# A decoder block on one core: the up projection by Strassen's seven products, and what is rearranged around it

## The chip, the cores and the metric

The kernel runs on one core of a Trainium2 chip. The metric is the device time of one execution in microseconds (us). Its engines are named as in the profile: PE is TensorE's matmul, PEld its weight load, DVE is VectorE, ACT is ScalarE, POOL is GpSimd, SP is SyncE, which issues most of the loads. "L127" is line 127 of the kernel before.

## What is computed

One decoder block on 512 tokens of width 1024 in float32: a gated merge of differential attention and causal pooling, an output projection, and an MLP with squared ReLU.

```python
h = rmsnorm(x, norm_attn_g[l])
u = h @ w_in[l]
u_q, u_k, u_v, u_pool, u_gate = jnp.split(u, splits, axis=-1)
...
a = diff_attention(q, k, v, positions, lam, subln_g[l], lam_init)
p = multiscale_pool(u_pool, w_pool[l], pool_scale[l])
gates = jax.nn.sigmoid(u_gate.reshape(B, S, N_BRANCHES, D_MODEL))
merged = gates[:, :, 0] * a + gates[:, :, 1] * p
x = x + (merged @ w_out[l]).astype(x.dtype)
h2 = rmsnorm(x, norm_mlp_g[l])
z = jnp.square(jax.nn.relu(h2 @ w_up[l]))
x = x + (z @ w_down[l]).astype(x.dtype)
return rmsnorm(x, final_norm_g)
```

`w_up` is 1024 x 4096 and `w_down` 4096 x 1024.

## The kernel before

**Numbers in two parts.** Every matmul takes operands of the type fp32r. To keep the accuracy, each operand is split: a high part (a cast on ACT) and a low part, the rest (a subtraction, mostly on DVE). A product is then three matmuls: high by high, high by low, low by high. Weights come as raw tiles of 128 x 1024 float32 (512 KB) through the SP queue (`load_w`, L95, three raw buffers with the tag `wr`), and `split_w` (L107) makes `wh` and `wl` (four buffers each). `get_w` (L112) can also make the low part with a DMA that accumulates ("dma": a cast, a negated copy and a transfer on POOL's queue that adds the raw weights).

**Order.** The program is written stage by stage. A planner orders the instructions of each engine by a simulated timeline and sets all waits; `after(later, earlier)` (L59) adds an edge to the planner's order and no wait on the chip.

**Attention.** Per head, projections, scores, softmax and values follow one another (`qk`, `attn`), and between them "fillers" (pooling and gate projections, `pool` at L409 and `gate` at L442) run. `merge` (L446) joins a head's output, its gates and its pooling product `pp`. `pool` loads its small weight `wpr` (L434) into a buffer with the tag `sq`, which the squares and norms of the heads use as well. Pooling, gate and `pp` products share three PSUM banks in turn.

**Output projection.** `w_out` comes in eight tiles in two halves (L546 to L563). After the second half of a tile of 128 tokens, the row scale is worked out, h2 is made (`h2`, all four token tiles), transposed on PE, and split into `x1gh` and `x1gl` (L571, L572).

**MLP.** D_FF is worked through in four quarters of 1024 columns; in each, `up(q)` (L606) and then `down(q)` (L620).

- `up` is a plain product: eight column tiles of 128, each 24 matmuls (`mm3`, L123) of 512 tokens, so 192 matmuls a quarter. In quarter 0 the first two tiles run in halves of 256 tokens, since the later tokens' h2 comes late. `z_of` (L588) takes relu and square on ACT, makes the forms of z that Strassen's scheme (Winograd's variant) wants (S1 to S4 by subtractions on DVE) and splits all seven into `zfh` and `zfl`, which hold seven forms each.
- `down` is already done by seven products over blocks (tokens in two halves, D_FF quarter in two halves, model width in two halves). Each product is 24 matmuls of 512 columns. The sums of weight blocks are made in DRAM-to-SBUF transfers that accumulate (`plus`, L638, on POOL's queue). The order is A11, S3, S2, S1, A12, S4, A22. Some products go onto banks that hold an earlier one (`onto`): S2 onto A11's, S4 onto S1's, A22 onto S3's. In between stands at least one other product. `to_x1` (L656) adds or subtracts the two banks of a product to `x1` on DVE. A sum U over the quarters is kept and added in the last one.
- In the last quarter the final norm is folded into the end (L686 to L730): the last product A22 runs in three pieces (`cols`, L708), 512, 256 and 256 columns, the second and third in the two halves of one bank.

## Time and profile before

| | us |
|---|---|
| three runs | 697.95, 695.3, 697.5; median 697.5 |
| the profiled execution | 697.38 |
| its span | 695.6 |
| last matmul of the last product starts | 688.30 |

The profile shows one execution. Its span runs from the first to the last instruction; the execution's own time has 1.8 us around it. Busy times of PE are not pure work: matmuls overlap, so that the distance between two starts, not the length of one, tells what a matmul costs.

### The profile page before, as it was taken

To read this page: it belongs to the slowest core of one execution; us is meant where nothing else is said; L and a number is where in the kernel's file an instruction comes from. 1 tells how busy PE (TensorE), PEld (TensorE's weight loads), DVE (VectorE), ACT (ScalarE), POOL (GpSimd) and SP (SyncE) were. 2 spreads that over 40 slices of the span, in tenths; PEclk is the share of its full clock that TensorE was granted. 3 is DMA by queue.
4 is the path that set the end of the run, shared out by engine and by line. 5 is a ranking of instruction groups with operands and counts; after the bars stand their busy time and mean duration, and the time that the engine had idled before them with its cause. 6 is when DMAs were issued, how large, how long until landed. Compare 5 with 4: busy or idle time off the path is not lost.

```text
span 695.6 us, 8855 instructions
## 1 busy us (share of the span) xinstructions
PE 679.3 (98%) x3158; PEld 564.3 (81%) x3158; DVE 476.4 (68%) x834; ACT 420.0 (60%) x683; POOL 161.2 (23%) x151
## 2 busy tenths in 40 slices
PE   8999999999999999999999999999999999999995
PEld 7788878888888887787888888888888888888884
DVE  6953977789788875965385675555765567645785
ACT  7554487977986689674356644455434554355544
POOL 6101634264345525532300010000210011000100
PEclk9999999999999999999999999999999999999998
DMA  7534574426436365345943269823797249952523
GB/s 268 165 115 116 133 150 120 103 63 157 125 88 151 99 152 121 91 163 201 246 128 118 91 107 288 231 100 91 179 247 209 90 92 209 248 177 91 95 57 122
DMA packets 30140, 100.88 MB, mean 145 GB/s; under 512 B 3600, under 2 KB 4240, under 8 KB 30096
## 3 DMA queue, kind: packets, MB, share of 16 engines
q1 hardware_dynamic: 22464, 72.79, 30.0%
q0 software_dynamic: 7488, 27.27, 23.0%
q8 instruction: 25, 0.41, 0.2%
q10 hardware_dynamic: 144, 0.26, 0.1%
q14 instruction: 19, 0.16, 0.1%
HBM read 98.20 MB, written 2.10 MB: 144 GB/s over the span
## 4 chain that ended last, share of the span: by engine, by line
PE 78%; DVE 10%; ACT 6%; issue 2%; DMA 2%; POOL 1%; SPq 0%; DVEq 0%; ACTq 0%; POOLq 0%
PE pu L127 8%; PE pu L128 8%; PE pu L131 8%; PE m L652 7%; PE m L653 7%; PE m L651 7%; PE po L536 2%; PE po L537 2%; PE po L538 2%; DVE p L376 2%; PE q L127 2%; PE k L127 2%; PE k L128 2%; PE q L128 2%; PE q L131 2%
## 5 line engine op out<-in xcount | busy, mean ns | idle before, releaser
L127 PE MATMUL pu<-x1gh,wh_up 128*128 128x512 f32 (+1 forms) x272 | 101.0, 377 | 0.2 <-ACT x1gh L571 0.2
L128 PE MATMUL pu<-x1gl,wh_up 128*128 128x512 f32 (+1 forms) x272 | 101.1, 377 | 0.0
L641 POOL DMA_DIRECT2D wr_b<-w_dn x32 | 27.7, 927 | 299.7 <-DVE wl_t L109 228.5
L109 DVE TENSOR_TENSOR wl_up<-wr_up,wh_up 128x1024 fp32r<-128x1024 f32 x32 | 39.2, 1225 | 41.8 <-ACT wh_up L108 30.3
L131 PE MATMUL pu<-x1gh,wl_up 128*128 128x512 f32 (+1 forms) x272 | 64.0, 377 | 0.0
L108 ACT CAST wh_up<-wr_up 128x1024 fp32r<-128x1024 f32 x32 | 33.7, 1053 | 44.4 <-PE m L653 20.0
L127 PEld LDWEIGHTS pu<-x1gh,wh_up 128*128 128x128 f32 x272 | 51.0, 188 | 9.8 <-ACT x1gh L571 0.5
L128 PEld LDWEIGHTS pu<-x1gl,wh_up 128*128 128x128 f32 x272 | 51.2, 188 | 9.6 <-DVE x1gl L572 0.2
L131 PEld LDWEIGHTS pu<-x1gh,wl_up 128*128 128x128 f32 x272 | 49.2, 188 | 9.3
L108 ACT CAST wh_t<-wr_b 128x1024 fp32r<-128x1024 f32 x32 | 33.6, 1053 | 38.1 <-PE m L653 24.6
L109 DVE TENSOR_TENSOR wl_t<-wr_b,wh_t 128x1024 fp32r<-128x1024 f32 x32 | 38.9, 1224 | 22.8 <-ACT wh_t L108 13.2
L604 DVE TENSOR_TENSOR zfl<-zr,zfh 128x512 fp32r<-128x512 f32 (+1 forms) x32 | 34.9, 1091 | 26.8 <-ACT zfh L603 26.8
L651 PE MATMUL m<-wh_t,zfh 128*128 128x512 f32 x120 | 46.7, 389 | 0.0
L652 PE MATMUL m<-wl_t,zfh 128*128 128x512 f32 x120 | 46.7, 389 | 0.0
L653 PE MATMUL m<-wh_t,zfl 128*128 128x512 f32 x120 | 46.7, 389 | 0.0
L371 ACT ACTIVATE p<-p,st 128x128 f32<-128x128 f32 (+3 forms) x64 | 35.8, 560 | 17.6 <-DVE st L367 17.1
L603 ACT CAST zfh<-zr 128x512 fp32r<-128x512 f32 (+1 forms) x32 | 30.2, 944 | 23.6 <-DVE zr L601 16.6
L652 PE MATMUL m<-wl_b,zfh 128*128 128x512 f32 x96 | 37.3, 389 | 0.0
L653 PE MATMUL m<-wh_b,zfl 128*128 128x512 f32 x96 | 37.3, 389 | 0.0
L651 PE MATMUL m<-wh_b,zfh 128*128 128x512 f32 x96 | 37.2, 389 | 0.0
L376 DVE SCALAR_TENSOR_TENSOR p<-p,st 128x128 f32<-128x128 f32 (+3 forms) x32 | 28.9, 902 | 8.0 <-ACT p L375 8.0
L109 DVE TENSOR_TENSOR wl_b<-wr_b,wh_b 128x1024 fp32r<-128x1024 f32 x16 | 19.6, 1224 | 18.4 <-PE pu L131 9.9
(266 smaller groups left out, 1794.4 us busy)
## 6 DMA issues: line engine op xcount, KB each, us to landing
wr_b<-w_dn SPq DMA_DIRECT2D x32, 512.0 KB, 3.8
wr_up<-w_up SPq DMA_DIRECT2D x32, 512.0 KB, 6.2
wr_b<-w_dn POOLq DMA_DIRECT2D x32, 512.0 KB, 5.9
wr_q<-w_in SPq DMA_DIRECT2D x8, 512.0 KB, 3.2
wr_k<-w_in SPq DMA_DIRECT2D x8, 512.0 KB, 3.3
wr_ga<-w_in SPq DMA_DIRECT2D x8, 512.0 KB, 3.2
wr_gp<-w_in SPq DMA_DIRECT2D x8, 512.0 KB, 3.4
wl_ga<-w_in POOLq DMA_DIRECT2D x8, 512.0 KB, 5.7
```

Source lines behind the costliest of these rows:

```text
L108: ins = A.copy(out=hi[:, sl], in_=raw[:, sl])
L109: (eng or G).tensor_tensor(out=lo[:, sl], in0=raw[:, sl], in1=f(hi)[:, sl], op=ALU.subtract)
L127: T.matmul(acc, lhsT=hi[:, c], rhs=rh[:, k, :], start=k == 0, stop=False)
L128: T.matmul(acc, lhsT=hi[:, c], rhs=rl[:, k, :], start=False, stop=False)
L131: T.matmul(acc, lhsT=lo[:, c], rhs=rh[:, k, :], start=False, stop=k == NK - 1)
L371: A.activation(out=pr[:, c, :N], in_=pr[:, c, :N], func=AF.Exp, scale=-1.0, bias=st[:, c : c + 1], accum_out=st[:, 2 + c : 3 + c])
L376: V.scalar_tensor_tensor(out=pr[:, 0, :N], in0=pr[:, 0, :N], scalar=st[:, 4:5], in1=pr[:, 1, :N], op0=ALU.mult, op1=ALU.add)
L603: A.copy(out=zfh[:, sl, p, :], in_=F[:, sl])
L604: V.tensor_tensor(out=zfl[:, sl, p, :], in0=F[:, sl], in1=f(zfh)[:, sl, p, :], op=ALU.subtract)
L651: T.matmul(pa[a], lhsT=zh, rhs=hi[:, sl], start=p == 0 and onto is None, stop=False, skip_group_check=True)
L652: T.matmul(pa[a], lhsT=zh, rhs=lo[:, sl], start=False, stop=False, skip_group_check=True)
L653: T.matmul(pa[a], lhsT=zl, rhs=hi[:, sl], start=False, stop=p == 3 and stop, skip_group_check=True)
```

## The change

- **Up in quarters 1 to 3** is done by seven products as well. Both operands are cut in two by two blocks: h2 (features in two halves, tokens in two halves), and the quarter of `w_up` (features in two halves, columns in two halves). A product of blocks has 2 x 2 x 12 matmuls of 256 columns (tokens). `w_up` is laid out anew by the host for it. Quarter 0 stays a plain product (`up_plain`), with weights in the new layout.
- **Forms of h2.** The four combined forms S1 to S4 of h2 are made once, during quarter 0 (`forms_h2`), and kept with their splits in `gss`; the plain blocks are in `gab`.
- **Forms of weights.** `weights` serves both projections. It loads block 0 (`r11`) and block 1 (`al`), adds them on DVE (`ga`), and changes `ga` and `al` step by step by accumulating transfers. Splits go into a ring of three pairs (two in `wp`, the third in `bk`). For some forms the cast is put behind the first matmul of the product before (`hold`).
- **Forms of z** live in a ring of four buffers (`zform`) in place of seven. `up` makes z blocks by keeping, joining, relu and square, in five raw blocks `R`; the forms are split as they come, the last three (S4, S3, A22) when down's products have set a buffer free.
- **Down** runs in the order S1, A11, S2, A12, S4, S3, A22 with S2, S3 and A22 on A11's banks one after the other, and S4 on S1's. U is gone: each product is added to or subtracted from `x1` as it stands. A product runs over the token tiles outside and the four parts inside.
- **The end:** the pieces for tokens 0 to 255 are finished earlier; the third piece of the last product has a bank of its own.
- **Before the MLP:** `wpr` has a tag of its own; `pp` of heads 4 to 7 is put behind the sigmoid in the planner's order; the raw ring has two buffers, and a third from the attention pool while that is open; the constants come in two transfers; the even tiles of `w_out`, whose low parts POOL made before, get them by an accumulating transfer in the first half and on DVE in the second; h2 is kept for two token tiles.

```diff
     def load_w(src, name, nsplit=1, parts=None):
-        raw = wp.tile([P, 1024], F32, tag="wr", name=f"wr_{name}", bufs=3)
+        nraw[0] += 1
+        third = nraw[0] % 3 == 0 and ctx1_open
+        raw = (tp if third else wp).tile([P, 1024], F32, tag="wr3" if third else "wr", name=f"wr_{name}", bufs=1 if third else 2)
...
-        wr = tmp("sq", f"wpr{g}", (P, 256))
+        wr = tmp("wpr", f"wpr{g}", (P, 256), bufs=1)
...
-        T.matmul(p_, lhsT=wph[:, c], rhs=dh, start=True, stop=False)
+        first_ = T.matmul(p_, lhsT=wph[:, c], rhs=dh, start=True, stop=False)
+        if h > 3:
+            after(first_, sg)
...
-        w = get_w(w_out[0, kk], f"o0_{kk}", V if kk % 2 else None)
+        w = get_w(w_out[0, kk], f"o0_{kk}", V if kk % 2 else "dma")
...
+    def forms_h2():
...
+        def minus(x, y):
+
+            V.tensor_tensor(out=w, in0=x[0], in1=y[0], op=ALU.subtract)
+            V.tensor_tensor(out=u, in0=x[1], in1=y[1], op=ALU.subtract)
+            V.tensor_tensor(out=w, in0=w, in1=u, op=ALU.add)
+
+        def less(x):
+
+            V.scalar_tensor_tensor(out=w, in0=w, scalar=-1.0, in1=x[0], op0=ALU.mult, op1=ALU.subtract)
+            V.tensor_tensor(out=w, in0=w, in1=x[1], op=ALU.subtract)
+
+        def parts(form):
+            hi, lo = gf[form]
+            A.copy(out=hi, in_=w)
+            V.tensor_tensor(out=lo, in0=w, in1=f(hi), op=ALU.subtract)
+
+        minus(a11, a21)
+        parts(S3)
+        minus(a22, a21)
+        parts(S1)
+        less(a11)
+        parts(S2)
+        less(a12)
+        parts(S4)
...
+        r11, al, ga = raw(0), raw(1, "wal", bk), raw(None, "wga", bk)
+        for c in range(2):
+            V.tensor_tensor(out=ga[c], in0=r11[c], in1=al[c], op=ALU.add)
+        for n, form in enumerate(order):
+            if n == 1:
+                plus(al, 3)
+            if form == A11:
+                yield parts(r11, "b11")
+            elif form == A12:
+                yield parts(raw(2), "b21")
+            elif form == S4:
+                yield parts(raw(3), "b22")
+            elif form == S3:
+                yield parts(al, "t3", first[-1])
+            else:
+                w = parts(ga, f"t{form}", None if form == S1 else first[-1])
+                if form != A22:
+                    plus(ga, {S1: 3, S2: 2}[form])
+                yield w
...
+    def zsplit(q, form, r, c=None):
+
+        if not c:
+            zform[form] = zf(f"z{form}_{q}")
+        z, sl = zform[form], slice(0, 4) if c is None else slice(2 * c, 2 * c + 2)
+        A.copy(out=z[:, 0, sl], in_=r[:, sl])
+        V.tensor_tensor(out=z[:, 1, sl], in0=r[:, sl], in1=f(z[:, 0, sl]), op=ALU.subtract)
...
+    def up(q):
+
+        W = weights(w_up, q, "u", (A11, S1, S2, S3, A22, A12, S4))
+
+        def product(form, name, onto=None):
...
+            for i in range(2):
+                hi, lo = w[i]
+                for p in range(2):
+                    a_ = pa[i][:, p * HS : p * HS + HS]
+                    for k in range(4):
...
+        ma = product(A11, "m1")
+        keep(ma, R[0])
+        mc = product(S1, "m5")
+        keep(mc, R[2])
+        product(S2, "m6", onto=ma)
+        keep(ma, R[1])
+        product(S3, "m7", onto=ma)
+        join(ma, R[2])
+        z_of(R[2], -1.0)
+        product(A22, "m4", onto=ma)
+        z_of(R[3], 1.0, ma)
+        sub(4, 2, 3)
+        zsplit(q, S1, R[4])
+        join(product(A12, "m2"), R[0])
+        z_of(R[0], 1.0)
+        zsplit(q, A11, R[0])
+        sub(4, 4, 0, neg=True)
+        zsplit(q, S2, R[4])
+        product(S4, "m3", onto=mc)
+        join(mc, R[1])
+        z_of(R[1], -1.0)
+        zsplit(q, A12, R[1])
...
+    def down(q):
+        W = weights(w_dn, q, "d", (S1, A11, S2, A12, S4, S3, A22))
...
+        mc = product(S1, "m5")
+        to_x1(mc, 1, 1)
+        ma = product(A11, "m1")
+        to_x1(ma, 0, 0)
+        product(S2, "m6", onto=ma)
...
+        to_x1(ma, 0, 1)
+        to_x1(product(A12, "m2"), 0, 0)
+        complete(0, 0)
+        product(S4, "m3", onto=mc)
+        to_x1(mc, 0, 1)
...
+        product(S3, "m7", onto=ma)
+        to_x1(ma, 1, 1)
         if not last:
-            to_x1(product(A22, w4, "m4", onto=m7), 1, 0)
+            product(A22, "m4", onto=ma)
+            to_x1(ma, 1, 0)
             return
...
+        for a, c0, c1 in ((0, 0, 512), (1, 0, 256), (1, 256, 512)):
+            t, a_ = 2 + a, acc("dm4b")[:, :256] if c0 else ma[a][:, c0:c1]
```

## What the change will do to the time

> **What bounds the kernel now.** I read the page's totals first, then the busy time by windows, then what TensorE waited for.
>
> ```profile
> span 695.6 us, 8855 instructions
> PE 679.3 (98%) x3158; PEld 564.3 (81%) x3158; DVE 476.4 (68%) x834; ACT 420.0 (60%) x683; POOL 161.2 (23%) x151
> PEclk9999999999999999999999999999999999999998
> ```
> ```profile
> 0.00:40.00 40.00, 36.81 (x162) 30.27 (x163) 29.41 (x70) 25.80 (x47) 14.74 (x24) 1.00 0.60 201
> 240.00:280.00 40.00, 38.65 (x187) 32.20 (x187) 26.03 (x70) 36.21 (x66) 17.03 (x16) 1.00 0.57 132
> 280.00:320.00 40.00, 37.05 (x177) 30.06 (x176) 29.15 (x53) 24.87 (x44) 14.72 (x10) 1.00 0.42 135
> 320.00:360.00 40.00, 39.90 (x193) 33.26 (x192) 24.25 (x42) 18.58 (x38) 8.87 (x6) 1.00 0.68 191
> 400.00:440.00 40.00, 40.00 (x178) 33.12 (x177) 25.64 (x30) 18.27 (x21) 6.89 (x8) 1.00 0.81 198
> 440.00:480.00 40.00, 40.00 (x178) 33.12 (x177) 22.12 (x28) 21.67 (x27) 0.00 (x0) 1.00 0.47 145
> 680.00:696.00 16.00, 7.45 (x43) 6.27 (x42) 8.04 (x24) 7.77 (x26) 0.00 (x0) 0.85 0.34 131
> ```
> The columns of a window are its bounds and length, then PE, PEld, DVE, ACT and POOL busy, granted clock, DMA share and GB/s. In the MLP (from about 357 us to 682) TensorE is busy 40.00 of 40 us at full clock, while VectorE holds 22 to 26 of 40. There only fewer or shorter matmuls can shorten the kernel. What TensorE loses lies at the start, in 240 to 320 us and in the tail:
>
> ```profile
> PE v L217 <- ACT xh L175: 1.9, 1, 1.9
> PE ga L127 <- DVE g L458: 1.4, 1, 1.4
> PE t L380 <- DVE p L376: 1.2, 1, 1.2
> ...
> PE m L715 <- DVE x L719: 1.1, 1, 1.1
> PE pp L455 <- ACT wt L438: 1.1, 1, 1.1
> PE po L536 <- DVE g L458: 0.6, 1, 0.6
> ```
>
> **The matmuls.** A group's mean length overstates a matmul, since neighbours overlap; what counts is the distance of starts. The first two rows are from the chain that ended last (8 matmuls of 512 columns end each block of 24), the others from the timeline (256 columns):
>
> ```profile
> 445.85 1.81 PE pu L131 x8
> 451.29 1.81 PE pu L131 x8
> ```
> ```profile
> 357.50 0.28 PE L127 MATMUL pu<-x1gh,wh_up 128*128 128x256 f32 x1
> ...
> 359.42 1.12 PE L131 MATMUL pu<-x1gh,wl_up 128*128 128x256 f32 x8
> 360.38 0.28 PE L127 MATMUL pu<-x1gh,wh_up 128*128 128x256 f32 x1
> ```
> A block of 24 at 512 columns takes 5.44 us, 226.7 ns each. A block of 24 at 256 columns takes 360.38 - 357.50 = 2.88 us, 120.0 ns each; its weight loads keep up. So halving the columns costs 6%.
>
> Up projection of a quarter before: 8 blocks, 8 x 5.44 = 43.5 us. After, in quarters 1 to 3: seven products of 2 x 2 x 12 = 48 matmuls of 256 columns, 336 x 0.1200 = 40.3 us. The gain is 3.2 us a quarter, **9.6 us** in three. Quarter 0 keeps 192 matmuls, a part of them as halves, as before. Down keeps 168 of 512 columns a quarter, 38.1 us. An eighth of the products is saved, and nearly half of that eighth is paid back by the shorter matmul.
>
> The Trainium skill, page "TensorE: Matmul & The Clock Gate", section "Back-to-back issue gap", gives N/2.4 + 2.5 ns, so 109.2 ns for 256 columns and 215.8 for 512; by that the saving would be an estimated 4.7 us a quarter, 14.2 in all. The trace has 120.0 and 226.7 at these very shapes, and the sum goes by them.
>
> **What VectorE and ScalarE take over.** Durations from the groups of 400 to 640 us:
>
> ```profile
> L109 DVE TENSOR_TENSOR wl_up<-wr_up,wh_up 128x1024 fp32r<-128x1024 f32 x24 | 29.4, 1225 | 34.9 <-ACT wh_up L108 23.7 <-PE pu L131 11.2
> L660 DVE TENSOR_TENSOR x<-x,m 128x512 f32<-128x512 f32 x36 | 23.2, 679 | 0.0
> L604 DVE TENSOR_TENSOR zfl<-zr,zfh 128x1280 fp32r<-128x1280 f32 x11 | 16.4, 1490 | 11.1 <-ACT zfh L603 11.1
> L604 DVE TENSOR_TENSOR zfl<-zr,zfh 128x512 fp32r<-128x512 f32 x12 | 8.3, 693 | 8.2 <-ACT zfh L603 8.2
> L595 DVE TENSOR_TENSOR zr<-zr 128x256 f32<-128x256 f32 x12 | 5.1, 425 | 0.1
> L108 ACT CAST wh_up<-wr_up 128x1024 fp32r<-128x1024 f32 x24 | 25.3, 1053 | 38.1 <-PE m L653 20.0 <-DMA wr_up<-w_up 13.4 <-PE pu L128 4.7
> L591 ACT ACTIVATE accu<-pu 128x512 f32<-128x512 f32 x23 | 13.8, 599 | 12.5 <-PE pu L131 12.5
> L594 ACT ACTIVATE zr<-accu 128x512 f32<-128x512 f32 x12 | 7.6, 634 | 0.4
> ```
> A quarter 1 to 3 after, on VectorE: 28 weight splits and 4 sums `ga` (32 x 1.225 = 39.2), 4 differences and 7 low parts of z (11 x 1.225 = 13.5, by the row of the same width), 6 joins and 14 evictions to `x1` (20 x 0.68 = 13.6): **66.3 us of 78.4**, 85%. ScalarE: 35 casts (36.9), 6 keeps (3.6) and 8 pairs of relu and square (9.9), 50.4 us. Both fit in total; I cost them at nothing in these quarters, with TensorE as the cover. If that cover is gone it is VectorE's queue that is late, below.
>
> Quarter 0 is worse. Its up stage now also makes four forms of h2: 14 operations of 1024 columns, 14 x 1.225 = 17.2 us of VectorE.
>
> ```profile
> 366.00:409.50 43.50, 43.50 (x215) 36.85 (x214) 25.34 (x35) 26.71 (x34) 1.71 (x2) 1.00 0.35 97
> 160.00:240.00 80.00, 80.00 (x386) 66.92 (x385) 69.33 (x146) 59.23 (x115) 36.97 (x31) 1.00 0.46 120
> 280.00:300.00 20.00, 18.75 (x93) 15.43 (x92) 19.07 (x38) 11.72 (x27) 11.01 (x8) 1.00 0.31 79
> ```
> VectorE now does 25.3 us in that stretch. Out go four rounds of `z_of` (4 x (4 x 0.425 + 0.693 + 1.490) = 15.5), in come 16 operations of 512 columns on z (11.1), the forms (17.2) and two sums for down (2.5): 40.6 of 43.5 us, 93%. The nearest rows: at 69.33 of 80 us (87%) TensorE loses nothing, at 19.07 of 20 (95%) it loses 1.25, or 6.25%. I take the latter for quarter 0: 43.5 x 0.0625 = **2.7 us lost** (bounds: nothing, as at 87%, and 5, twice that), and the former for quarters 1 to 3.
>
> **DMA and queues.**
>
> ```profile
> q1 hardware_dynamic: 22464, 72.79, 30.0%
> q0 software_dynamic: 7488, 27.27, 23.0%
> ```
> ```profile
> wr_b<-w_dn POOLq DMA_DIRECT2D x24, 512.0 KB, 5.9
> wr_b<-w_dn SPq DMA_DIRECT2D x24, 512.0 KB, 3.5
> wr_up<-w_up SPq DMA_DIRECT2D x24, 512.0 KB, 6.6
> ```
> The 52 accumulating transfers (32 of `w_dn`, 20 of `w_in`) took 23% of the span, 3.1 us each of all engines; a plain one, 156 in 30%, about 1.3. A quarter goes from 18 plain and 8 accumulating (49 us in 81.6) to 16 and 12 (58 in 78.4, 74%). The window 400:440 had 0.81 with TensorE full, so I cost it at nothing. The `ga` chain (split S1, add block 3, split S2, add block 2, split A22) needs about 1 + 5.9 + 3.5 = 10.4 us a link. S1 may be split two products before it runs (three pairs of split buffers), which gives 5.8 + 5.8 us and a little more. Behind a raw load that waits for its buffer on SP stand the next projection's first loads; on POOL only the next accumulate.
>
> **The banks.** Down now runs S2 straight onto A11's banks and A22 onto S3's; up runs S3 onto S2's and A22 onto S3's. Before, another product lay between. The eviction of bank 0 has the 12 matmuls of bank 1 for cover: 12 x 0.2267 = 2.72 us in down, 24 x 0.12 = 2.88 in up. It needs 0.68 us and at most one operation of 1.2 us ahead of it: hidden. With two ahead, 2 x 1.225 + 0.68 = 3.13: 0.4 us late. The same bank matters as a whole, as the tail shows:
>
> ```profile
> 686.88 0.39 PE L715 MATMUL m<-wh_t,zfh 128*128 128x256 f32 x1 [1.14 <-DVE x L719]
> ```
> The third piece of the last product waits there for an eviction of the other half of its bank. (The Trainium skill, "PSUM — Partial Sum Buffer", section "Terms", says that TensorE and another engine may not be on one bank at once; by it every chained product is such a wait, and this row agrees.) The change gives that piece a bank of its own: **-1.1 us**; bounds nothing (ScalarE's queue in the tail may hold it) and 1.8 (its scaling of 0.7 us leaves the queue).
>
> **Attention.** `wpr` gets a tag of its own.
>
> ```profile
> 309.24 7.64 DMA wpr<-w_pool
> ```
> This load waited for a shared buffer and then ran among others; the two waits behind it (`pp` 1.1, `po` 0.6) go when it is loaded early: **-1.7 us**. Bounds: -3.1 if the wait of `ga` (1.4) goes too through the new order behind the sigmoid, +2 if what is late next is `w_out`, whose even tiles now take an accumulate (5.9) in place of POOL's subtraction. The other edits there have one answer: the constants loaded in two pieces, two raw buffers in place of three after attention, two `w_out` splits moved from POOL to VectorE (2.5 us) and h2 kept for two token tiles cost nothing, since VectorE holds 24 of the 40 us from 320 to 360 while TensorE is full.
>
> **Sum.** The profiled execution took 697.4 us (span 695.6 and 1.8 around it), the median being 697.5. 697.4 - 9.6 - 1.1 - 1.7 + 2.7 = **687.7 us**.
>
> **Rivals.**
> 1. *VectorE paces quarters 1 to 3 too.* 63 instructions a quarter share 78.4 - 66.3 = 12.1 us: from 0.19 us of waiting per instruction on, evictions, splits and z forms are late and chained banks pass it on. For it: 280:300. Against: 160:240 at 87%. Price: 6.25% of 3 x 78.4 = 14.7 us, 702.4. It cancels the gain from 4.1% on. This is the case that ends slower.
> 2. *Weights late between up and down.* A12, S4 and down's first block share one pair of raw tiles. After S4's split come a load (3.5 to 6.6), the sum, a cast and a low part (3.5 together), 7.0 to 10.1 us, against a product of 5.76: 1.3 to 4.3 us three times, 691.5 to 700.7, middle 696. For it: one queue, SP, holds all raw loads. Against: S4's split can be done ahead of its product.
> 3. *Nothing lost in quarter 0, and the three attention waits gone:* 697.4 - 9.6 - 1.1 - 3.1 = 683.6.
> 4. *A 256-column matmul at half of 226.7 ns in steady state:* 336 x 0.1133 = 38.1, 16.3 us saved, 681.0. The row of 120.0 ns speaks against it.
> The number of matmuls is fixed by the code, so that the change does nothing is none.
>
> **Chances.** Forecast 0.53 (own range 684.5 to 692), rival 1 0.13, rival 2 0.20, rival 3 0.12, rival 4 0.02. A measurement tells about 0.5%, 3.5 us, from no change: faster is the forecast, rivals 3 and 4 and a quarter of rival 2, 0.72; same is the rest of rival 2, 0.15; slower 0.13. The range 682.5 to 697 leaves out rival 1, the upper end of rival 2, and rival 4.
>
> **What would show it.** Starts of `pu` matmuls 120 ns apart in quarters 1 to 3 and a period near 78.4 us confirm the first term; gaps on TensorE between 366 and 410 us, ended by VectorE, the loss in quarter 0; gaps ended by an eviction at a chained product rival 1; gaps ended by a split just as down begins rival 2. No wait of `pp` on `wt` would confirm the attention term. I am wrong if TensorE is below 98% busy in quarters 1 to 3, or if starts there are further apart than 120 ns.

## The result, and the profile after

The change made the kernel slower by half a per cent: 700.83 us (median of six executions, 698.99 to 702.70) against 697.42 (695.30 to 697.95), a ratio of 1.0054 with a 95% interval of 1.0033 to 1.0075. The prediction was 687.7, with a range to 697: wrong in sign, and outside its range. The profiled execution took 700.6.

From here on L numbers are lines of the changed kernel: L112 and L113 split a weight (cast on ScalarE, low part on VectorE), L694 and L695 split z the same way, L778 and L779 are its relu and square, L819 to L822 the three matmuls of down. A tile `wh_d...` or `wl_d...` with a t holds a sum of weight blocks, with a b a single block. The page after, its totals:

```profile
span 698.8 us, 9783 instructions
PE 678.3 (97%) x3590; PEld 581.6 (83%) x3590; DVE 519.1 (74%) x853; ACT 446.1 (64%) x723; POOL 161.8 (23%) x159
```

The busy time by windows, cut where a projection begins (columns as in the prediction):

```profile
402.00:440.00 38.00, 38.00 (x184) 32.10 (x184) 34.68 (x40) 19.71 (x23) 4.67 (x6) 1.00 0.63 173
440.00:480.00 40.00, 40.00 (x320) 39.31 (x319) 25.57 (x26) 25.65 (x34) 5.69 (x7) 1.00 0.80 196
480.00:520.00 40.00, 37.64 (x170) 30.79 (x169) 35.16 (x39) 20.74 (x23) 3.68 (x5) 0.96 0.61 160
563.00:606.00 43.00, 41.18 (x194) 34.35 (x193) 35.97 (x38) 21.07 (x23) 5.18 (x6) 0.96 0.65 168
646.00:686.00 40.00, 36.02 (x146) 27.78 (x147) 32.49 (x40) 22.37 (x33) 1.73 (x2) 0.96 0.45 107
```

The first row is down of quarter 0, the second up of quarter 1: TensorE is full. Down of quarters 1, 2 and 3 (down 1 to down 3 from here on), the last three rows, is where it stands idle, and where the granted clock falls below 1. Starts of the first matmul of each stage give the balance, before and then after:

| stretch | before, us | after, us | difference | predicted |
|---|---|---|---|---|
| to the start of up 0 | 357.50 | 354.74 | -2.8 | -1.7 |
| up 0 | 46.47 | 47.07 | +0.6 | +2.7 |
| down 0 and up 1 | 81.60 | 78.43 | -3.2 | -3.2 |
| down 1 and up 2 | 81.6 | 83.02 | +1.4 | -3.2 |
| down 2 and up 3 | 81.6 | 82.64 | +1.0 | -3.2 |
| down 3 to the start of its last product | 32.6 | 39.73 | +7.1 | 0 |
| last product to the end of the span | 14.18 | 13.19 | -1.0 | -1.1 |

The sum is +3.2, the difference of the spans (698.8 and 695.6). The terms of the prediction are there. What is not in its sum is 4.6 + 4.2 + 7.1 = 15.9 us lost in three downs: TensorE's waits there come to 8.4 us, and most of the rest is a slower clock behind them (last section). What TensorE waited for, from 400 us on (total, times, longest):

```profile
PE dm L821 <- DVE z L695: 4.3, 3, 1.9
PE dm L819 <- ACT wh_db L112: 3.1, 1, 3.1
PE dm L819 <- ACT z L694: 1.0, 3, 0.5
```

In the first and the third row it waits for z, with VectorE or ScalarE named as the last link. The second row, the longest single wait, is in down 3 and for A12's weights. Both engines had been idle before, so the cause lies further back. The chain that ended last, in order of time (start, length, what), goes through down 1:

```profile
475.43 1.14 DVE wl_dt L113
476.58 0.28 issue
476.86 9.37 DMA wga_dNone<-w_dn
486.30 1.06 ACT wh_dt L112
487.39 1.23 DVE wl_dt L113
...
493.22 1.15 DVE z L695
494.40 0.50 PE dm L821
```

And ScalarE's timeline beside it (start, length, operation, and in brackets the idle time before it with what ended it):

```profile
480.02 1.04 ACT L112 CAST wh_dt<-wga_dNone 128x1024 fp32r<-128x1024 f32 x1
486.30 1.05 ACT L112 CAST wh_dt<-wga_dNone 128x1024 fp32r<-128x1024 f32 x1 [5.25 <-DMA wga_dNone<-w_dn]
487.26 0.63 ACT L779 ACTIVATE rawz<-rawz 128x512 f32<-128x512 f32 x1
487.79 0.62 ACT L778 ACTIVATE rawz<-rawz 128x512 f32<-128x512 f32 x1
488.31 1.04 ACT L694 CAST z<-rawz 128x1024 fp32r<-128x1024 f32 x1
```

VectorE at the same place:

```profile
487.39 1.23 DVE L113 TENSOR_TENSOR wl_dt<-wga_dNone,wh_dt 128x1024 fp32r<-128x1024 f32 x1 [3.35 <-ACT wh_dt L112]
```

This is the story of the loss. TensorE runs the product A12 before S2, but the casts of S2's weights stand ahead of A12's z on ScalarE. The second of them waits 5.25 us for an accumulating transfer that took 9.37 us. Behind it stand the relu, the square and the casts of z for the next products, whose data are there; VectorE in turn waits for the cast, 3.35 us, and then has a backlog. So z is late for A12. The casts of S2's weights wait 4.71 us in down 2 and 4.24 and 2.76 us in down 3; there the casts of A12's weights stand behind them too, and begin at 659.92 us, 8 us after the first of the raw tiles landed.

The transfer is slow in a burst with which down begins: two raw tiles of A12's weights, two accumulates of `al` (the sum for S3, the sixth product) and two of `ga` (the sum for S2) are issued within 9 us (469.62 to 478.33 in down 1). Over the whole execution the medians look harmless (copies, KB each, median us to landing):

```profile
wr_d<-w_dn SPq DMA_DIRECT2D x24, 512.0 KB, 3.6
wga_dNone<-w_dn POOLq DMA_DIRECT2D x16, 512.0 KB, 5.7
wga_uNone<-w_up POOLq DMA_DIRECT2D x12, 512.0 KB, 7.9
```

### The profile page after: what moved, and what is told of

Same layout as the page of the kernel before. It is cut to its first block, busy times and chain, and to the rows that moved or that the text cites. A ratio compares the mean times of both kernels' runs of the same rounds, so it can differ in the third digit from the quotient of the medians.

```text
span 698.8 us, 9783 instructions
## 1 busy us (share of the span) xinstructions
PE 678.3 (97%) x3590; PEld 581.6 (83%) x3590; DVE 519.1 (74%) x853; ACT 446.1 (64%) x723; POOL 161.8 (23%) x159
## 4 chain that ended last, share of the span: by engine, by line
PE 68%; DVE 13%; DMA 8%; ACT 6%; issue 4%; POOL 1%; SPq 0%; ACTq 0%; POOLq 0%; DVEq 0%
PE pu L726 5%; PE dm L821 5%; PE dm L822 5%; PE dm L819 5%; DMA wga_dNone<-w_dn 3%; PE um L760 3%; PE um L762 3%; PE um L765 3%; PE v L220 2%; PE v L221 2%; PE v L222 2%; DMA wga_uNone<-w_up 2%; PE po L557 2%; PE po L558 2%; PE po L559 2%
## 5 line engine op out<-in xcount | busy, mean ns | idle before, releaser
L821 PE MATMUL dm<-wh_dt,z 128*128 128x512 f32 (+1 forms) x128 | 49.6, 387 | 0.1
L822 PE MATMUL dm<-wl_dt,z 128*128 128x512 f32 (+1 forms) x128 | 49.2, 386 | 0.0
L819 PE MATMUL dm<-wh_dt,z 128*128 128x512 f32 (+1 forms) x128 | 48.9, 388 | 0.3 <-ACT z L694 0.3
L837 DVE TENSOR_TENSOR x<-x,dm 128x512 f32<-128x512 f32 x54 | 36.3, 681 | 15.0 <-PE dm L822 14.9
L112 ACT CAST wh_ut<-wga_uNone 128x1024 fp32r<-128x1024 f32 x18 | 18.9, 1050 | 43.3 <-DMA wga_uNone<-w_up 32.5
L821 PE MATMUL dm<-wh_db,z 128*128 128x512 f32 x96 | 39.3, 417 | 4.3 <-DVE z L695 4.3
L819 PE MATMUL dm<-wh_db,z 128*128 128x512 f32 x96 | 38.2, 409 | 3.8 <-ACT wh_db L112 3.1
L112 ACT CAST wh_dt<-wga_dNone 128x1024 fp32r<-128x1024 f32 x24 | 24.9, 1047 | 22.7 <-DMA wga_dNone<-w_dn 17.6
L113 DVE TENSOR_TENSOR wl_ut<-wga_uNone,wh_ut 128x1024 fp32r<-128x1024 f32 x18 | 22.0, 1223 | 23.2 <-ACT wh_ut L112 23.2
L113 DVE TENSOR_TENSOR wl_dt<-wga_dNone,wh_dt 128x1024 fp32r<-128x1024 f32 x24 | 28.9, 1219 | 13.3 <-ACT wh_dt L112 13.3
L822 PE MATMUL dm<-wl_db,z 128*128 128x512 f32 x96 | 38.0, 408 | 0.0
L112 ACT CAST wh_db<-wr_d 128x1024 fp32r<-128x1024 f32 x24 | 25.0, 1045 | 19.2 <-DMA wr_d<-w_dn 17.8
L760 PE MATMUL um<-gss,wh_ut 128*128 128x256 f32 x144 | 36.1, 283 | 0.0
L762 PE MATMUL um<-gss,wh_ut 128*128 128x256 f32 x144 | 36.1, 283 | 0.0
L113 DVE TENSOR_TENSOR wl_db<-wr_d,wh_db 128x1024 fp32r<-128x1024 f32 x24 | 29.1, 1218 | 7.2 <-PE pu L726 4.5
L695 DVE TENSOR_TENSOR z<-rawz,z 128x1024 fp32r<-128x1024 f32 (+1 forms) x32 | 34.2, 1084 | 0.0
L726 PE MATMUL pu<-gab,wh_up 128*128 128x512 f32 (+1 forms) x160 | 31.7, 349 | 0.6 <-DVE gab L596 0.4
L372 DVE CUSTOM_DVE_ANT_0 p<-s,mask 128x128 f32<-128x128 f32 (+3 forms) x64 | 29.8, 482 | 2.0 <-PE s L371 2.0
L694 ACT CAST z<-rawz 128x1024 fp32r<-128x1024 f32 (+1 forms) x32 | 29.3, 937 | 2.9 <-PE dm L822 1.2
```

The lines of the kernel that those rows point to most:

```text
L112: ins = A.copy(out=hi[:, sl], in_=raw[:, sl])
L113: (eng or G).tensor_tensor(out=lo[:, sl], in0=raw[:, sl], in1=f(hi)[:, sl], op=ALU.subtract)
L372: V.tensor_tensor_reduce(out=pr[:, c, :N], in0=s_[:, :N], in1=mask[:, S - N :], scale=-0.125, scalar=-NEG, op0=ALU.add, op1=ALU.min, accum ...
L695: V.tensor_tensor(out=z[:, 1, sl], in0=r[:, sl], in1=f(z[:, 0, sl]), op=ALU.subtract)
L726: T.matmul(a_, lhsT=w[k // 4][part][:, c_], rhs=gab[k // 4][:, ts[0] : ts[1], i, k % 4, :], start=k + i + part == 0, stop=part == 1 and k ...
L760: m = T.matmul(a_, lhsT=hi[:, c], rhs=rh[:, k, :], start=p + k == 0 and onto is None, stop=False, skip_group_check=True)
```

## The experiments

Theory A: a cast that waits for a late transfer stands ahead of z in ScalarE's queue, and that order is what costs. Theory B: VectorE paces quarters 1 to 3 (rival 1 of the prediction). Theory C, formed on the way: the burst makes whatever is cast first late, in any order. Times are medians; a ratio is to the kernel before on the same chip.

| kernel | us | ratio and its 95% interval |
|---|---|---|
| the change | 700.8 | 1.0054 (1.0033 to 1.0075) |
| e1 `al` behind `ga` | 695.2 | 0.9958 (0.9939 to 0.9977) |
| e2 S2's casts behind A12's z | 692.5 | 0.9937 (0.9920 to 0.9953) |
| e3 both | 693.9 | 0.9947 (0.9931 to 0.9964) |
| e4 `wpr` in its old buffer | 702.7 | one execution |
| e5 e2, A11's casts behind z of S1 | 696.1 | 0.9990 (0.9970 to 1.0009) |
| e6 e5, `al` late in up | 692.7 | 0.9938 (0.9922 to 0.9954) |
| e7 e2, more VectorE work | 704.0 | 1.0114 (1.0088 to 1.0141) |
| e8 e5, gains late | 694.5 | 0.9966 (0.9948 to 0.9984) |
| e9 A12 written ahead of S2 | 697.3 | 0.9998 (0.9989 to 1.0007) |
| e10 e9, `al` late in up | 695.0 | 0.9967 (0.9955 to 0.9978) |
| e11 e9, `al` behind `ga` | 692.2 | 0.9935 (0.9922 to 0.9948) |
| e12 e10, A11's casts behind z of S1 | 699.7 | 1.0033 (1.0016 to 1.0050) |
| e13 `al` behind `ga`, another edit | 691.8 | 0.9928 (0.9913 to 0.9942) |
| e14 e13, A12 ahead of S2 | 699.7 | 1.0040 (1.0023 to 1.0058) |
| e15 e14, `al` late in up | 698.9 | 1.0032 (1.0019 to 1.0045) |
| **e16** e15, A12's casts behind z of S2 | 686.9 | 0.9860 (0.9841 to 0.9879) |
| **e17** e9, A12's casts behind z of S2 | 688.2 | 0.9877 (0.9862 to 0.9891) |
| e18 `al` last | 708.3 | 1.0171 (1.0154 to 1.0189) |

### First round: the order of transfers, and the order of casts (e1 to e4)

e1, in `plus`: only POOL's order of issue changes; TensorE, ScalarE, VectorE and SP run the instructions of the changed kernel in its order.

```diff
-                G.dma_start(out=tiles[c], in_=src[q, b, c], accum_op=ALU.add)
+                ins = G.dma_start(out=tiles[c], in_=src[q, b, c], accum_op=ALU.add)
+                if nm == "d" and tiles is al:
+                    after(ins, state["ga"])
+                state["ga"] = ins
```

> Only POOL's order in down changes: the accumulates into al (needed by S3, sixth product) go behind the first accumulates into ga (needed by S2). Theory A (a burst of transfers makes the second ga tile land late, 9.4 us after its issue in quarter 1 and 13.1 in quarter 3, and ScalarE, which stands at the cast of that tile, holds back the square and casts of A12's z, for which TensorE then waits): ga lands within about 6 us of its issue, the waits of 2.4, 1.8 and 3.6 us in the three downs shrink below 0.5 us, the slower clock behind them goes, and the time is about 688 us (686 to 692). Theory B (VectorE is full and paces quarters 1 to 3): nothing that VectorE does changes, so the time stays at 700 to 702 us.

e2, in `parts` and `zsplit`: SP and POOL keep the change's order of issue. VectorE's low parts and some of TensorE's matmuls move along with the casts, as the planner orders anew.

```diff
                 if hold:
                     after(cast, hold)
+                if nm == "d" and b == f"t{S2}":
+                    after(cast, state["zc", q, A12])
...
-        A.copy(out=z[:, 0, sl], in_=r[:, sl])
+        state["zc", q, form] = A.copy(out=z[:, 0, sl], in_=r[:, sl])
```

> Only the planner's order on ScalarE in down is bound: the casts of S2's weights go behind the cast of A12's z (and what follows from it in the planner's order). The transfers are issued as before. Theory A: ga lands as late as before, but the squares and casts of z stand ahead of the cast that waits for it, so TensorE's waits for z go; where ga lands latest (quarter 3) A12's weights, which stand behind S2's casts, still wait 1 to 2 us. Time 687 to 692 us. Theory B: 700 to 702 us.

e3 is both edits.

> Both edits. Theory A: no wait above 0.5 us in the three downs, periods of 78.4 us from down to down, 685 to 688 us. Theory B: 700 to 702 us.

e4 gives `wpr` its old shared buffer back: `wr = tmp("sq", f"wpr{g}", (P, 256))`.

> Undo of one part of the attention edits: wpr shares the tag sq again. If the early load of wpr is what removed the waits behind it (pp on wt 1.1 us and po on g 0.6 us before), the first matmul of the up projection starts about 1.7 us later than in the changed kernel (354.7 us), near 356.4. If other edits removed them (the order behind the sigmoid, the transfers of w_out), it stays at 354 to 355 us.

Either edit alone gets back more than the loss against the kernel before: 5.6 us in e1, 8.3 in e2. VectorE has the same instructions in both, in e1 in the same order too, so theory B falls as the cause. But e1 and e3 missed their ranges by 3 and 6 us, e2 its own by 0.5, and the two together are not better than e2. ScalarE's wait for the accumulates of down went from 17.6 us to 5.2 in e1, yet other casts now wait. (e1's ten executions spread from 691.3 to 696.5, and the profiled one is the fastest.) First the changed kernel, then e1 (ScalarE's waits, from 400 us on):

```profile
ACT wh_ut L112 <- DMA wga_uNone<-w_up: 32.5, 9, 9.3
ACT wh_db L112 <- DMA wr_d<-w_dn: 17.8, 5, 5.6
ACT wh_dt L112 <- DMA wga_dNone<-w_dn: 17.6, 5, 5.2
```
```profile
ACT wh_db L112 <- DMA wr_d<-w_dn: 27.2, 5, 6.7
```

e4: up 0 starts at 356.09, 1.35 us later than with the new buffer, and the two waits behind `wpr` are back, together 0.2 us smaller than before the change:

```profile
PE pp L460 <- ACT wt L443: 0.9, 1, 0.9
PE po L557 <- DVE g L465: 0.6, 1, 0.6
```

### Second round: what is left, and VectorE's margin (e5 to e8)

e5 is e2 with one more order in `parts`: A11's weights are cast behind z of S1.

```diff
+                if nm == "d" and b == "b11":
+                    after(cast, state["zc", q, S1])
```

> e2 with one more order on ScalarE: down's casts of A11's weights (second product) wait until z of S1 (first product) is cast. Theory A (a cast that waits for a transfer holds up what stands behind it on ScalarE, here the z of the first product of down): the gaps ended by z at the start of down, 1.11 us in quarter 2 and 1.66 in quarter 3 of e2, go, and the slow clock after the longer one: 692.5 - 1.1 - 1.7 - 0.5 = about 689.5 (688 to 691). Rival 2 of the prediction (the raw tile pair shared by A12, S4 and down's first block makes the weights late): the gaps stay and are now ended by wh_dt, 692.5 (692 to 693.5).

e6 is e5 with `al` issued in up behind S1's accumulates (the `after` of e1 for up, and `plus(al, 3)` one product later).

> e5 with al's accumulates of up behind those of S1 on POOL as well. Theory A: wh_ut is waited for less on ScalarE (32.5 us in the changed kernel), the gaps ended by wh_ub in up (0.19 and 0.63 us in e2) go: 0.5 to 1 us below e5, about 688.8 (687.5 to 690.5). Rival: al itself is then late for S3, the fourth product: a gap of 1 to 3 us ended by wh_ut in each of three quarters, 691 to 697.

e7 is e2 with the low part of each second weight tile of down made twice:

```diff
+                if nm == "d" and q and c:
+                    V.tensor_tensor(out=lo, in0=rs[c], in1=f(hi), op=ALU.subtract)
```

> e2 with the low part of each second weight tile of down made twice in quarters 1 to 3: 21 more VectorE instructions of 1.23 us, 25.8 us. Rival 1 of the prediction (VectorE paces quarters 1 to 3): nearly all of it shows, 15 to 26 us above e2, 708 to 718. Theory A (VectorE has room, ScalarE's queue and the transfers behind it set the loss): 0 to 4 us above e2, 692.5 to 696.5.

e8 is e5 with the load of the final gains behind the raw tiles of A12 (`after(ins, state["raw"])` in `gain`, called after A12's product).

> e5 with the final gains loaded behind the raw tiles of A12 in the last down, out of the burst at its start. Theory A: transfers in that burst land 1 to 2 us sooner, but z no longer stands behind them: 0 to 1 us below e5. Rival (the burst itself, not what stands behind it, sets the loss in quarter 3, the largest of the three): 2 us or more below e5.

e5 is a miss: 3.5 us slower than e2, not 3 faster. The waits for z at the start of down did go; another took their place (TensorE's waits in e5, whose profiled execution is the slowest of its twelve):

```profile
PE dm L826 <- DVE wl_db L113: 7.0, 3, 2.7
```

Those are A12's weights. A11's casts now free the pair of raw tiles later: the loads of A12's go out 1.0 and 2.7 us after down 1 begins, in place of 6.3 and 2.3 before it in e2. Their casts stand behind those of S2 as well. The order of one cast had only moved the wait. e6 and e8 got 3.4 and 1.6 us back from e5: more than theory A had said of e6 (0.5 to 1), and between the two theories for e8. What part of their edits did that was not traced, and twelve executions of e5 spread over 8.7 us.

e7 decides on neither side: 25.8 us of work cost 11.5 us. By stages, against e2: +4.3 in down 1 with up 2, -1.2 in down 2 with up 3, +8.2 in the last down, where 8.6 us were added. There VectorE is full (e7, the last down):

```profile
645.00:694.00 49.00, 42.43 (x184) 33.02 (x183) 47.22 (x65) 27.48 (x47) 3.48 (x4) 0.97 0.46 109
```

So the 17.2 us added in quarters 1 and 2 cost 3.1: VectorE has much of the room there that the prediction gave it, and in the last down it has none to spare. (Repeating instructions also shifts the planner's orders, so the stages cannot be read finer than this.)

### Third round: A12 written ahead of S2 (e9 to e12)

```diff
-        W = weights(w_dn, q, "d", (S1, A11, S2, A12, S4, S3, A22))
+        W = weights(w_dn, q, "d", (S1, A11, A12, S2, S4, S3, A22))
```

and the line of A12's product moved ahead of S2's. ScalarE's order then has S2's casts behind all four z.

> The changed kernel with A12's product written ahead of S2's in down, as TensorE runs them already: the split of A12's weights and its z then stand ahead of S2's casts on ScalarE and VectorE. Theory A (a cast that waits for its transfer holds up what stands behind it): in e2, e5 and e8 the casts of A12's weights still stood behind those of S2, and gaps of 1 to 2.75 us ended by wl_db followed; they go with those ended by z, and left are 1 to 2 us at the start of each down: 689.5 (688 to 691.5). Rival (the burst of transfers makes S2's weights late for TensorE itself, in whatever order they are cast): the gaps move to S2's product, ended by wh_dt, 692 to 697.

> e9 with al's accumulates of up behind those of S1 on POOL. Theory A: the waits of ScalarE for wga_u in up are shorter and the gaps ended by wh_ub go, 0 to 1.5 us below e9, 688.5 (687 to 690.5). Rival: al is then late for S3 in up, 1 to 3 us above e9.

> e9 with al's accumulates of down behind the first ones of ga, the edit of e1. Theory A: S2's weights land sooner, but in e9 nothing that TensorE waits for stands behind their casts: within 1 us of e9. Rival (the landing of S2's weights still sets the time): 2 us or more below e9.

> e10 with the casts of A11's weights in down behind z of S1, the edit of e5. Theory A: the gaps ended by z at the start of down go as they went in e5, 1 to 2 us below e10, 687.5 (686 to 689.5). Rival 2 of the prediction (one pair of raw tiles makes the weights late between up and down): A11's weights are then late, as e5 at 696.1 was slower than e2; 2 us or more above e10.

e9 is the second miss, 697.3 in place of 689.5, and e11 contradicts theory A as it stood: `al` later is worth 5.1 us with S2's casts out of the way. ScalarE's timeline in e9, down 1, shows how:

```profile
475.60 0.63 ACT L778 ACTIVATE rawz<-rawz 128x512 f32<-128x512 f32 x1
481.58 1.05 ACT L112 CAST wh_db<-wr_d 128x1024 fp32r<-128x1024 f32 x1 [5.36 <-DMA wr_d<-w_dn]
482.54 0.63 ACT L779 ACTIVATE rawz<-rawz 128x512 f32<-128x512 f32 x1
```

Now it is the cast of A12's own raw tile that stands ahead of z and waits. Its load is a plain one, 3.6 us at the median of the changed kernel, but it went out with the burst and took 8.93 us. The place that waits has changed, the mechanism has not. e10's later `al` in up is worth 2.4 us. e12, 4.7 us slower than e10, shows again that A11's casts may not be delayed. That is the size that rival 2 had said, but TensorE waits for z there (8.8 us from 400 us on), not for weights.

### Fourth round: order or landing (e13 to e16)

e13 orders `al`'s accumulates of down `after` the first matmul of A11:

```diff
-            if n == 1:
-                plus(al, 3)
+            if n == (2 if nm == "d" else 1):
+                plus(al, 3, first[-1] if nm == "d" else None)
```

> The changed kernel with al's accumulates of down held until TensorE begins the second product (A11), out of the burst; the casts of S2's weights stand ahead of A12's z as in the changed kernel. Theory C (the burst makes the transfers late, and any cast that stands first waits for them): the landing of S2's accumulates falls to about 5.5 us and A12's raw loads to about 3.5, gaps go whatever the order: 691.5 (689.5 to 693.5). Theory A (the order of casts sets it): the casts still stand ahead, most of the gain is missing, 695 to 699. Rival: al is late for S3, a gap of 1 to 3 us ended by wh_dt in the sixth product, 695 to 702.

> e13 with A12 written ahead of S2 in down, as in e9 (697.3). Theory C: as e13, within 1.5 us, and about 5 us below e9. Theory A: 2 us or more below e13.

> e14 with al's accumulates of up behind those of S1 as in e10. Theory C: the same in up, 1 to 2.5 us below e14 as e10 was 2.4 below e9: 689.5 (687.5 to 691.5). Rival: with the burst of down gone nothing in up is late, the same as e14 within 0.7.

e16 adds one order to e15, in `parts`:

```diff
+                if nm == "d" and b == "b21":
+                    after(cast, state["zc", q, S2])
```

> e15 with the casts of A12's weights in down behind z of S2. Theory C: without the burst their transfers are there when the casts come, and the order is worth little: within 1 us of e15. Theory A: 1 to 3 us below e15.

e13's edit did not hold the accumulates: an `after` between two queues makes no wait, and they went out right behind those of `ga`, at 475.8 us in e16, before down 1 began at 479.1. So e13 and e14 are kin of e1 and e11, not the test of theory C that was meant. e13 is 2 to 3 us faster than e1 with the same order of transfers, which is not explained. And e14, which both theories had near e13 or below it, is 7.5 us slower than e11. In down 1 and down 2 ScalarE's order differs in the place of one cast: the second of A12's weights stands ahead of a relu and a square that z needs in e14, and behind them in e11. In e14, down 1, it holds them up for 4.03 us:

```profile
486.91 1.05 ACT L112 CAST wh_db<-wr_d 128x1024 fp32r<-128x1024 f32 x1 [4.03 <-DMA wr_d<-w_dn]
487.86 0.63 ACT L780 ACTIVATE rawz<-rawz 128x512 f32<-128x512 f32 x1
```

e15 to e16 is the clean pair. The edit is one order on ScalarE, the transfers are issued in the same order, and the raw tile of A12 lands at the same time in both (8.6 us and 8.7 us after its issue, at 485.45 and 485.48 us). It takes 686.9 in place of 698.9: 12 us, more than either theory had said (within 1, and 1 to 3). ScalarE in down 1, first e15, then e16, where work that is ready fills part of the wait:

```profile
485.53 1.05 ACT L112 CAST wh_db<-wr_d 128x1024 fp32r<-128x1024 f32 x1 [3.49 <-DMA wr_d<-w_dn]
486.48 0.63 ACT L783 ACTIVATE rawz<-rawz 128x512 f32<-128x512 f32 x1
487.01 1.04 ACT L699 CAST z<-rawz 128x1024 fp32r<-128x1024 f32 x1
```
```profile
481.44 1.04 ACT L701 CAST z<-rawz 128x1024 fp32r<-128x1024 f32 x1
485.56 1.05 ACT L112 CAST wh_db<-wr_d 128x1024 fp32r<-128x1024 f32 x1 [2.13 <-DMA wr_d<-w_dn]
```

VectorE's low part of that weight tile moves behind z's as well, so the pair shows what the order of the splits is worth, cast and low part together; the two were not separated.

### Fifth round: each alone (e17, e18)

e17 is e9 with that same order of e16, and `al` where the change has it.

> Only ScalarE's order: the changed kernel with A12 written ahead of S2 in down and the casts of A12's weights behind z of S2; al's accumulates stay where the changed kernel has them, in the burst. Theory A (a waiting cast ahead of z is what costs): most of e16's gain is there, 688.5 (686.5 to 691). Theory C (the late landing of the burst costs whatever the order): e9's 697.3 or e14's 699.7, 695 or more.

e18 is e9 with `al` of down issued behind S2's accumulates (`plus(al, 3)` after `plus(ga, 2)`, and the `after` of e1).

> Only the transfers: e14 (699.7), whose casts of A12's weights stand ahead of z, with al's accumulates of down behind S2's on POOL, out of the burst for good (in e14 they were issued right behind the first ones of ga, since an order written in the code binds only instructions of one queue). If late landing is needed for the loss as well as the order, A12's raw tiles land in 4 to 6 us in place of 8.8, the gaps ended by z go and it takes 691 (688.5 to 693.5). If the order alone does it, 697 or more. If al is then late for S3, gaps ended by wh_dt in the sixth product, 693 to 700.

e17 settles it for theory A: 688.2, and the edit against e9 (697.3) is the order of casts alone, with the low parts following as in e16. SP and POOL issue their transfers in the same order in the changed kernel, in e2, e9 and e17. ScalarE's timeline in down 1 of e17: one wait is left, 2.11 us. Three of the four z casts with which down 1 begins are done before it; the fourth (487.68) still comes in time for A12's product, which begins at 491.2 us:

```profile
482.63 1.04 ACT L696 CAST z<-rawz 128x1024 fp32r<-128x1024 f32 x1
483.57 1.05 ACT L112 CAST wh_db<-wr_d 128x1024 fp32r<-128x1024 f32 x1
486.73 1.05 ACT L112 CAST wh_db<-wr_d 128x1024 fp32r<-128x1024 f32 x1 [2.11 <-DMA wr_d<-w_dn]
487.68 1.04 ACT L696 CAST z<-rawz 128x1024 fp32r<-128x1024 f32 x1
```

The accumulate of `ga` takes 9.96 us there, no less than in the changed kernel, and nothing is late in down 1. All that TensorE waits for from 400 us on, and the window of down 1 that lost 2.36 of 40 us in the changed kernel, in two halves:

```profile
PE dm L821 <- ACT z L696: 1.8, 2, 1.6
```
```profile
480.00:500.00 20.00, 20.00 (x91) 16.62 (x91) 19.50 (x21) 14.55 (x16) 1.73 (x2) 1.00 0.70 178
500.00:520.00 20.00, 20.00 (x110) 17.40 (x109) 16.68 (x18) 6.91 (x7) 3.45 (x4) 1.00 0.68 183
```

e18 is the other half, and a trade. With `al` gone from the burst, A12's raw tiles land in 4.3 and 5.1 us, its second cast waits 0.57 us in place of 4.03, and down 1 has no gap at A12's z. (In down 3, where two accumulates of `ga` and the load of the gains go out within 2 us, A12's raw tiles still take 8.0 and 7.3 us, a cast of them waits 3.78 us, and a gap of 1.4 us at A12's z is left.) But `al` then meets the second accumulates of `ga` and the first loads of up, lands in 10.9 to 14.0 us, and ScalarE waits for it. The 708.3 us are above what had been said for a late `al` (693 to 700). ScalarE in e18, from 400 us on:

```profile
ACT wh_dt L112 <- DMA wal_d<-w_dn: 35.2, 8, 7.7
```

So the loss at A12's z needs both, a late transfer and its split ahead of z, and theory C falls; but moving the transfer moves the trouble, and moving the cast removes it.

## Why the prediction was wrong

- **The matmuls (-9.6): right.** Down 0 with up 1 took 78.43 us, 3.2 less than before, and starts of 256 columns lie 0.120 us apart in steady state (478.81, 478.93, 479.05). The page "TensorE: Matmul & The Clock Gate" of the Trainium skill, section "Back-to-back issue gap", would have had an estimated 109 ns; the runs stay with the trace of before. In e17 the three periods are 78.4, 78.6 and 80.6 us.
- **The tail (-1.1): right.** From the start of the last product to the end of the span 13.19 us in place of 14.18, -1.0.
- **The banks (nothing): right.** From 400 us on no gap of TensorE in the changed kernel is ended by an eviction. S2 straight onto A11's banks did not arise: the planner ran A12 between them.
- **Attention (-1.7): right for its cause.** The waits of `pp` and `po` are gone, and e4 puts `wpr`'s buffer at 1.35, one execution against one (in the other 17 runs with the new buffer up 0 starts between 353.3 and 355.1 us, so its size is known to about 1 us). Up 0 starts 2.8 earlier in all. The wait for `xh` at the start is 1.3 shorter (1.9 before, 0.6 after), and that of `ga` (1.4) is gone too, the prediction's bound of -3.1; neither was examined.
- **Quarter 0 (+2.7): mis-sized**, +0.6 was measured. VectorE does 38.0 of 43.5 us in the same stretch (363.24 to 406.74 us), 87%, not the 40.6 that were summed up (93%); at 87% the prediction's own row lost nothing.
- **"Both fit in total; I cost them at nothing in these quarters, with TensorE as the cover": the step that failed.** The sums, 50.4 us for ScalarE and 66.3 for VectorE of 78.4, were somewhat high (45.8 and 60.7 in the period from down 0 to down 1, 47.3 and 62.6 in the next), so both did fit; what they cost is not in a sum. ScalarE was idle for 5 us with work at hand, because the instruction at the head of its queue waited for a transfer. The prediction asked what each queue holds behind a waiting load on SP and POOL, and did not ask it of ScalarE, where 24 of the 35 casts of a quarter take a tile that a transfer fills, and four more a sum of two such tiles. It priced this at nothing; it cost 15.9 us, of which e17 gets back 12.6 with no transfer issued in another order.
- **The `ga` chain "gives 5.8 + 5.8 us and a little more": wrong in its number, too.** It took the median landing of an accumulate, 5.9 us. The one that counts is issued in the burst and took 9.37. The trace of before could have told: 13 of its 32 accumulates of `w_dn` took more than 7 us, the longest 15.1. The share of the transfer engines over 40 us (0.81 with TensorE full) says nothing of a burst of 9 us.
- **Rival 1** gave 702.4, near the measured time, by luck. While TensorE stood idle in down 1 VectorE was indeed busy without a break (3.40 of 3.40 us, first window of the last section), but with what had piled up while it waited 3.35 us for ScalarE: it passed the delay on and did not start it. It is refuted as the cause by e1, e2 and e17, which leave VectorE its work. e7 shows that its margin is thin in the last down.
- **Rival 2** (weights late between up and down, 691.5 to 700.7) named the right class, work that waits for a late transfer. The place it named costs 1.6 us once, at the start of down 3 in e17; the same wait stands there in e2, e13 and e16 with 1.5 to 1.7. TensorE waits for z in it. It is still open whether the raw pair or the casts ahead of z make it.
- **Rival 3** had its two conditions nearly met (attention -2.8, quarter 0 +0.6), which the loss in the downs hid.

The version to keep is e16 or e17. At 686.9 and 688.2 us both beat the kernel before by 1.2 to 1.4%, and stand where the prediction's sum stood. That match is in part luck: in e17 the part before up 0 and quarter 0 came out 3.1 us better than forecast, and the three periods and down 3 3.4 us worse. But with its casts no longer blocking ScalarE the change was worth about what its terms said.

## What to carry to other kernels

Add up an engine's work, and then read its queue: for each instruction that waits for a transfer, name what stands behind it and who needs that next. Let work whose data are there go first, and the casts of late transfers behind it; here one such order was worth 8 to 12 us (e2, e16, e17), while other orders of the transfers brought between 9 us of gain (e13) and 11 of loss (e18 against e9). Price a transfer by the burst in which it is issued, not by its median.

## What was not expected of the hardware

- **The clock after a short gap.** After the two gaps in down 1 (0.50 and 1.86 us) the granted clock fell to half for about 3 us. The windows of the changed kernel around it, and TensorE's timeline inside:

```profile
491.00:494.40 3.40, 1.05 (x4) 0.30 (x2) 3.40 (x5) 1.71 (x2) 0.00 (x0) 1.00 0.83 152
495.00:498.00 3.00, 3.00 (x9) 2.32 (x8) 3.00 (x5) 1.20 (x2) 0.00 (x0) 0.52 0.78 262
498.00:501.00 3.00, 3.00 (x14) 2.44 (x13) 1.51 (x2) 2.80 (x3) 0.00 (x0) 0.92 0.38 116
```
```profile
491.81 0.73 PE L819 MATMUL dm<-wh_db,z 128*128 128x512 f32 x2 [0.50 <-ACT z L694]
494.40 0.50 PE L821 MATMUL dm<-wh_db,z 128*128 128x512 f32 x1 [1.86 <-DVE z L695]
...
495.74 0.63 PE L822 MATMUL dm<-wl_db,z 128*128 128x512 f32 x1
496.17 0.63 PE L819 MATMUL dm<-wh_db,z 128*128 128x512 f32 x1
```

  Starts 0.43 us apart in place of 0.227, for some seven matmuls: about 1.5 us. So the two gaps, 2.4 us, cost nearly 4, and 4.6 us were lost in that down. The other two downs have one such stretch each (577.1 to 580.4 and 662.4 to 665.7 us at 0.50), so that about 5 of the 15.9 us are clock. Not every gap is followed by one: after 2.75 us in down 1 of e5 the clock stayed at 1.00 (500.0 to 503.5 us), and after 1.66 us at the start of down 3 it fell to 0.50 in e11 (644.0 to 647.3 us) and stayed at 1.00 in e2 (643.0 to 648.0 us). What decides it is not shown. The Trainium skill, "TensorE: Matmul & The Clock Gate", section "Part 1: The HAM clock gate (the "warmup" mystery)", has the clock halved after an idle window of about 3.4 us; here 1.05 us of work within 3.4 did not prevent it.
- **Landing times in a burst.** From issue to landing a plain load of 512 KB took about 3.3 us alone and 7.9 to 9.5 among the accumulates at the start of the changed kernel's downs; an accumulate took about 5.3 alone and up to 13.1 there, 14.0 in down 1 of e18.
- **ScalarE does not pass its head of queue.** A cast waited 5.25 us with a relu, a square and a cast behind it whose inputs were complete. The same page of the Trainium skill, section "Architectural detail: the array is 16× 32×32, not 1× 128×128", says that ScalarE and VectorE take their instructions strictly first in, first out; the trace agrees.
